# A two-layer hybrid trunk: the last two output-projection passes in the same PSUM banks, the mean square later, the sums of x earlier

## The chip, the cores and the metric

One core of a Trainium2 chip runs the whole program. The metric is device time in microseconds (us) of one execution, the median of several runs. A profile of one further execution shows what each engine did: PE (TensorE matmul), PEld (TensorE weight load), DVE (VectorE), ACT (ScalarE), POOL (GpSimd) and SP (SyncE, which issues most of the transfers).

## The reference

The input is one sequence of 512 frames with 1024 channels in float32. Two layers follow each other; cut to what matters here:

```python
def _layer(x, ...):                                # x: (1, 512, 1024)
    z = _rms(x, norm1) @ w_in                      # 1024 -> 2572 columns
    ya = sliding-window attention of 8 heads
    yb = forgetting attention of 4 heads
    yc = mLSTM readout of 4 heads
    x = x + concat(ya, yb, yc) @ w_out             # 1024 -> 1024
    u = _rms(x, norm2) @ w_ff1                     # 1024 -> 4096
    return x + square(relu(u)) @ w_ff2             # 4096 -> 1024
```

The change touches the product with `w_out`, the root-mean-square norm after it, and the order of work at the start of the feed-forward part.

## The kernel before, in words

x is kept transposed in SBUF as `xT`: 8 tiles of 128 channels by 512 frames. All large products run in float32 precision on fp32r operands: each operand is split into a rounded part and a rest (`whi`, `wlo` for weights, `xh`, `xl` for x), and each product is three matmuls, hi by hi (L263), hi by lo (L264) and lo by hi (L265).

**Weights come as jobs.** A job is 128 x 1024 elements: SP transfers them into a raw buffer (`raw`, `fraw`, `xt`, `ms`; L158), ACT rounds them to `whi` (L205), DVE subtracts to get `wlo` (L206). There are three `whi`/`wlo` buffers, so a job can be prepared at the earliest when the job three places ahead of it has been used up. `getjob` hands the jobs out in a fixed order.

**Attention and projections** are interleaved: `big_work` is a generator that emits a bit of projection work at each step, and `fill` and `fill_to(mark)` draw from it between pieces of attention work. The output projection is its last part. It contracts over eight tiles of 128 rows, k = 0 to 7. Tiles 0 to 3 belong to the sliding-window heads, 4 and 5 to the forgetting heads, 6 and 7 to the mLSTM heads, which come last. So it runs in three passes over k (`WPASS`: 0-3, 4-5, 6-7), each over four pairs of output tiles (`hf` = 0 to 3). For each pair it takes two PSUM banks, accumulates the pass and adds the two banks to `xT` on DVE (L587). In the third pass the sum is complete, and `xprep` follows for each tile: ACT makes the rounded part of x times the gain (L334), DVE the rest (L335). `c_tail(1)` transposes the last mLSTM readout on PE (L1007, four transposes of `yt`, which POOL writes at L1000), and ACT and DVE split the result into tile k = 7 (L1008, L1009).

**The feed-forward part.** Its hidden 4096 columns are made in eight rounds. A plain round (`ff1_std`, rounds 0 and 1, set by `NSTD = 2` in line 46) uses four jobs of 48 matmuls of 128 x 256. The other rounds (`ff1_st`) use a scheme with seven products of blocks in place of eight, and so seven jobs of 24 matmuls; the second matrix (`ff2`) uses the same scheme throughout. The seven products need sums and differences of blocks of x, which `xsums` forms on DVE and ACT (L354 to L375). The norm is not applied to x beforehand: since relu(r u) squared is r squared times relu(u) squared, DVE multiplies `xT` by the mean square plus epsilon before the first addition of a block (L1291), adds the products (L1292), and multiplies by r squared at the end of the layer. `sqacc` forms the sum of squares of `xT` (ACT squares, DVE adds at L330), and `emit_r2` averages it over channels with one PE product against a matrix of 1/1024 (L1123, float32, 512 columns), takes it out of PSUM on DVE (L1125) and derives r squared (ACT L1128, L1129; DVE L1130, L1131).

The first eight steps are the eight jobs of the two plain rounds; from the ninth on, `ff_pairs` alternates a job of `ff2` with one of `ff1_st`. In the text below the jobs of the feed-forward part are numbered from 0, so 0 to 7 are plain and 8 is the first of `ff2`. The sum of squares is emitted after job 0, `xsums` after jobs 1 to 4, the average after job 3. A scheduler orders the instructions of each engine; each engine then works through its list in that order.

## Time and profile before

| | |
|---|---|
| time, median of 3 runs (lowest to highest) | 1066.45 us (1066.31 to 1067.0) |
| the profiled execution: its own time / its span | 1067.08 us / 1065.4 us |
| PE busy, matmuls | 1055.0 us (99%), 8764 |
| PEld busy | 1004.0 us (94%) |
| DVE busy | 904.2 us (85%) |
| ACT busy | 629.5 us (59%) |
| granted PE clock | 0.999 |

The span runs from the first to the last instruction; the time holds about 1.7 us more. A busy share is time in which at least one instruction of the engine is under way. Matmuls overlap each other, so one that is listed with 0.28 us occupies PE for less: how long each one really takes from the next is read from the starts of neighbours, or from how many fit into a stretch. Layer 0 has its output projection up to about 223 us and its feed-forward part from there to 535 us; layer 1 follows 525.8 us later with the same order of work.

### The profile page before, as it was taken

Reading aid. Unit: us, or ns where it says so; the run is one execution under the profiler, and the core shown is the slowest. Engines: PE = TensorE matmul, PEld = TensorE weight load, DVE = VectorE, ACT = ScalarE, POOL = GpSimd, SP = SyncE. Lnnn points to the kernel's source line nnn. Section 1 sums busy time; section 2 is a strip of 40 time slices with the busy share of each in tenths; the row PEclk is TensorE's granted clock in tenths of the full one; section 3 lists DMA queues with packets and bytes.
Section 4 is the critical chain, followed back from the end, with each engine's and each line's share of the span. In section 5 each row is a group of like instructions: output and inputs, shape, how many; then the busy total and the mean of one; then the engine's idle time right before and its main releaser. Section 6 shows DMA issues by size and latency. Waiting matters only on the chain.

```text
span 1065.4 us, 21677 instructions
## 1 busy us (share of the span) xinstructions
PE 1055.0 (99%) x8764; PEld 1004.0 (94%) x8764; DVE 904.2 (85%) x1540; ACT 629.5 (59%) x1097; POOL 102.3 (10%) x154
## 2 busy tenths in 40 slices
PE   8999999999999999999999999999999999999998
PEld 8999977899999999999999998778999999999998
DVE  7696877899997988988977878688999888898797
ACT  6446655376666666567455467444766666666662
POOL 2030020100010000010001200101000101001000
PEclk9999999999999999999999999999999999999999
DMA  6523121165388587677135221213544876777742
GB/s 214 161 102 110 60 68 50 61 191 146 119 209 225 160 217 199 176 203 196 51 110 163 95 80 41 87 43 136 143 120 140 221 208 177 225 180 187 220 128 80
DMA packets 47365, 151.86 MB, mean 143 GB/s; under 512 B 5648, under 2 KB 8848, under 8 KB 47264
## 3 DMA queue, kind: packets, MB, share of 16 engines
q1 hardware_dynamic: 39056, 120.84, 33.1%
q0 software_dynamic: 8064, 29.36, 15.6%
q8 instruction: 69, 1.13, 0.4%
q14 instruction: 32, 0.26, 0.1%
q10 hardware_dynamic: 144, 0.26, 0.1%
HBM read 147.86 MB, written 2.13 MB: 141 GB/s over the span
## 4 chain that ended last, share of the span: by engine, by line
PE 89%; DVE 7%; ACT 2%; issue 1%; DMA 0%; SPq 0%; DVEq 0%
PE at L263 27%; PE at L264 26%; PE at L265 26%; DVE rt L726 2%; DVE wlo L206 1%; PE at L856 1%; PE at L898 1%; PE at L756 1%; PE at L881 1%; PE at L979 1%; DVE z L728 1%; DVE z L722 1%; PE at L811 1%; PE at L789 1%; DMA raw<-in_w_in_dram 0%
## 5 line engine op out<-in xcount | busy, mean ns | idle before, releaser
L205 ACT ACTIVATE whi<-raw 128x1024 fp32r<-128x1024 f32 (+1 forms) x130 | 136.4, 1049 | 114.9 <-PE at L264 88.2
L264 PE MATMUL at<-xhl,whi 128*128 128x256 f32 (+1 forms) x704 | 198.7, 282 | 0.0
L263 PE MATMUL at<-xhl,whi 128*128 128x256 f32 (+1 forms) x640 | 181.9, 284 | 0.0
L265 PE MATMUL at<-xhl,wlo 128*128 128x256 f32 (+1 forms) x640 | 181.1, 283 | 0.0
L263 PE MATMUL at<-yg,whi 128*128 128x256 f32 (+1 forms) x592 | 179.9, 307 | 0.5 <-DVE xT L1292 0.5
L206 DVE TENSOR_TENSOR wlo<-raw,whi 128x1024 fp32r<-128x1024 f32 (+1 forms) x130 | 157.0, 1208 | 27.3 <-ACT whi L205 26.9
L265 PE MATMUL at<-yg,wlo 128*128 128x256 f32 (+1 forms) x592 | 178.4, 301 | 0.0
L264 PE MATMUL at<-yg,whi 128*128 128x256 f32 (+1 forms) x560 | 169.4, 303 | 0.0
L263 PE MATMUL at<-whi,xhl 128*128 128x256 f32 (+1 forms) x576 | 162.9, 283 | 1.2 <-ACT xhl L334 1.0
L265 PE MATMUL at<-whi,xhl 128*128 128x256 f32 (+1 forms) x576 | 160.4, 279 | 0.5 <-DVE xhl L335 0.5
L264 PE MATMUL at<-wlo,xhl 128*128 128x256 f32 (+1 forms) x576 | 160.3, 278 | 0.5 <-DVE wlo L206 0.5
L205 ACT ACTIVATE whi<-fraw 128x1024 fp32r<-128x1024 f32 x100 | 106.3, 1063 | 89.3 <-PE at L264 79.8
L206 DVE TENSOR_TENSOR wlo<-fraw,whi 128x1024 fp32r<-128x1024 f32 x100 | 122.1, 1221 | 27.1 <-ACT whi L205 26.6
L264 PEld LDWEIGHTS at<-xhl,whi 128*128 128x128 f32 x704 | 132.1, 188 | 1.9 <-issue 0.5
L265 PEld LDWEIGHTS at<-xhl,wlo 128*128 128x128 f32 x640 | 120.7, 189 | 1.2
L263 PEld LDWEIGHTS at<-xhl,whi 128*128 128x128 f32 x640 | 120.1, 188 | 1.8 <-ACT ct L1230 0.5
L263 PEld LDWEIGHTS at<-yg,whi 128*128 128x128 f32 x592 | 111.2, 188 | 6.3 <-issue 1.7
L265 PEld LDWEIGHTS at<-yg,wlo 128*128 128x128 f32 x592 | 111.1, 188 | 5.3
L263 PEld LDWEIGHTS at<-whi,xhl 128*128 128x128 f32 x576 | 108.3, 188 | 2.2 <-ACT xhl L334 1.2
L264 PEld LDWEIGHTS at<-yg,whi 128*128 128x128 f32 x560 | 105.3, 188 | 4.2 <-DVE yg L1009 0.5
L265 PEld LDWEIGHTS at<-whi,xhl 128*128 128x128 f32 x576 | 108.2, 188 | 1.0 <-DVE xhl L335 0.9
L264 PEld LDWEIGHTS at<-wlo,xhl 128*128 128x128 f32 x576 | 108.2, 188 | 0.7 <-DVE wlo L206 0.7
(299 smaller groups left out, 2516.8 us busy)
## 6 DMA issues: line engine op xcount, KB each, us to landing
fraw<-in_w_dram SPq DMA_DIRECT2D x72, 512.0 KB, 4.3
raw<-in_w_dram SPq DMA_DIRECT2D x56, 512.0 KB, 4.3
raw<-in_w_in_dram SPq DMA_DIRECT2D x34, 512.0 KB, 3.3
fraw<-in_w_dram POOLq DMA_DIRECT2D x32, 512.0 KB, 6.2
raw<-in_w_out_dram SPq DMA_DIRECT2D x16, 512.0 KB, 3.2
xt<-in_w_dram SPq DMA_DIRECT2D x16, 512.0 KB, 5.8
raw<-in_w_dram POOLq DMA_DIRECT2D x14, 512.0 KB, 7.4
ms<-in_w_dram SPq DMA_DIRECT2D x12, 512.0 KB, 4.3
```

The lines of the kernel that those rows point to most:

```text
L205: A.activation(hi[:, cs_], raw[:, cs_], AF.Copy)
L206: V.tensor_tensor(lo[:, cs_], raw[:, cs_], hi[:, cs_], ALU.subtract)
L263: T.matmul(o, sh, mh, start=first, stop=False, skip_group_check=skip)
L264: T.matmul(o, sh, ml, start=False, stop=False, skip_group_check=skip)
L265: T.matmul(o, sl, mh, start=False, stop=last, skip_group_check=skip)
L722: V.tensor_tensor(z10, z10, bc(rq), ALU.mult)
L726: V.tensor_tensor(r10[:, oo:oo + n, a:a + 32], z10[:, oo:oo + n, b:b + 32], tb(S_, n, a, a + 32), ALU.mult)
L728: V.tensor_tensor(zaq[t], ro[:, :640], rt[:, :640], ALU.add)
L756: T.matmul(sc[r][:, g * 256:g * 256 + nk], qTA[g][r * 64:(r + 1) * 64, c * P:(c + 1) * P], kTA[r * 64:(r + 1) * 64, k0:k0 + nk], start=Tru ...
L789: T.transpose(pt[:w, u * P:(u + 1) * P], pe[:, u, :w], ident)
L811: T.matmul(po[r * 64:(r + 1) * 64, g * P:(g + 1) * P], vt[:w, r * 64:(r + 1) * 64], p1[:w, u * P:(u + 1) * P], start=g == 0, stop=p2 is No ...
L856: T.matmul(sp[:, :nk], qTB[rs, pr, n * P:(n + 1) * P], kTB[rs, pr, :nk], start=True, stop=False)
```

## The change

Four things are altered, in both layers.

- **Output projection.** The first pass (k = 0 to 3) stays. The second and third share banks: pairs 0, 1 and 2 take k = 4 and 5, keep their six banks open, and take k = 6 and 7 later, in the order 2, 0, 1; pair 3 takes k = 4 to 7 at one go, last. Each pair is added to `xT` once for the two passes. The weights are laid out on the host so that the four jobs fit this order.
- **The last transposes** (`c_tail(1)`) come after k = 4 and 5 of pairs 0 and 1, no longer after those of all four pairs.
- **Sums of x first.** `xsums` is emitted after jobs 0 to 3, the sum of squares after job 4, the average (`emit_r2`) after job 7. The buffer `xt`, in which `xsums` works, goes to the weight transfers after job 4 in place of job 7. The last two operations on r squared (`finish_r2`) move behind the first seven products of `ff2`.
- **Bank choice.** `bank(True)`, used where ACT writes a bank before PE accumulates into it, takes a bank that has been used in this part before.

In words the change was also said to use one plain round of the first feed-forward matrix in place of two. In the code `NSTD` is 2 on both sides; the new loop is written with `NSTD`, and its value doesn't change.

```diff
@@ -570,26 +570,54 @@
                         DEST[gname](t, ps[t])
                 done.add(gname)
                 yield 1.31
-            for pi, (a, b) in enumerate(WPASS):
-                for hf in range(4):
-                    ps = [att() for _ in range(2)]
-                    if b - a == 4 or hf % 2 == 0:
-                        ws = getjob()
-                    for k in range(a, b):
-                        hi, lo = ws[k - a if b - a == 4 else hf % 2 * 2 + k - a]
-                        for j in range(2):
-                            cs_ = slice(j * P, (j + 1) * P)
-                            mm3(ps[j], hi[:, cs_], lo[:, cs_], yhi(k), ylo(k), k == a, k == b - 1)
-                        if k < b - 1:
-                            yield 1.31
-                    for j in range(2):
-                        kx = hf * 2 + j
-                        V.tensor_tensor(xT[:, kx], ps[j], xT[:, kx], ALU.add)
-                        if pi == len(WPASS) - 1:
-                            xprep(kx, g2(l, kx), xh, xl)
-                    if hf == 3:
-                        done.add(f"wo{pi}")
+            def wo_part(ps, tiles, k, first, stop):
+                hi, lo = tiles
+                for j in range(2):
+                    cs_ = slice(j * P, (j + 1) * P)
+                    mm3(ps[j], hi[:, cs_], lo[:, cs_], yhi(k), ylo(k), first, stop)
+
+            def wo_out(ps, hf, full):
+                for j in range(2):
+                    kx = hf * 2 + j
+                    V.tensor_tensor(xT[:, kx], ps[j], xT[:, kx], ALU.add)
+                    if full:
+                        xprep(kx, g2(l, kx), xh, xl)
+
+            for hf in range(4):
+                ps = [att() for _ in range(2)]
+                ws = getjob()
+                for k in range(4):
+                    wo_part(ps, ws[k], k, k == 0, k == 3)
+                    if k < 3:
+                        yield 1.31
+                wo_out(ps, hf, False)
+                if hf == 3:
+                    done.add("wo0")
+                yield 1.31
+            open_ = {}
+            for hf in range(3):
+                open_[hf] = [att() for _ in range(2)]
+                if hf != 1:
+                    ws = getjob()
+                for k in (4, 5):
+                    wo_part(open_[hf], ws[2 * (hf % 2) + k - 4], k, k == 4, False)
+                    if k == 5:
+                        done.add(f"wo1{hf}")
                     yield 1.31
+            for hf in (2, 0, 1, 3):
+                if hf == 3:
+                    open_[hf] = [att() for _ in range(2)]
+                if hf in (0, 3):
+                    ws = getjob()
+                for k in range(4 if hf == 3 else 6, 8):
+                    wo_part(open_[hf], ws[k - 4 if hf == 3 else (hf if hf < 2 else 1) * 2 + k - 6], k, hf == 3 and k == 4,
+                            k == 7)
+                    if k < 7:
+                        yield 1.31
+                wo_out(open_[hf], hf, True)
+                if hf == 3:
+                    done.add("wo2")
+                yield 1.31
         bw = big_work()
         credit = [0.0]
@@ -1091,8 +1119,9 @@
             fill(FB, "wo0")
         fill_to("wo0")
         c_tail(0)
-        fill_to("wo1")
+        fill_to("wo11")
         c_tail(1)
+        fill_to("wo12")
         close_phase()
         open_phase(FFP)
         pos["ff"] = l
@@ -1113,8 +1142,13 @@
         quads = [unit(xb(0, 1, t_)) for t_ in (xh, xl)]
         banks = deque(att() for _ in range(8))
-        def bank():
-            return banks.popleft()
+        full = set()
+
+        def bank(seeded=False):
+            b = next(b for b in banks if not seeded or id(b) in full)
+            banks.remove(b)
+            full.add(id(b))
+            return b
         rr_ = {}
@@ -1127,9 +1161,12 @@
             r2 = cst.tile([P, S], F32, tag="aux", name=f"r2{l}")
             A.activation(lnv, nv, AF.Ln, scale=-1.0)
             A.activation(r2, lnv, AF.Exp, scale=-1.0)
+            rr_.update(nv=nv, lnv=lnv, r2=r2)
+
+        def finish_r2():
+            nv, lnv, r2 = (rr_[n] for n in ("nv", "lnv", "r2"))
             V.tensor_tensor(lnv, nv, r2, ALU.mult)
             V.scalar_tensor_tensor(r2, lnv, 2.0, r2, ALU.add, ALU.mult)
-            rr_.update(nv=nv, r2=r2)
         def prod(bk, bh, bl, start, halves=None):
             ws = getjob()
...
@@ -1351,28 +1388,27 @@
                         xprep(kx, g1(l + 1, kx), xhA, xlA)
                 give(s, dg, "t")
                 if s == 0 and dg:
+                    finish_r2()
                     free_ff.append(ms_)
                 yield
         gens = {1: (None for r in range(NR) for _ in (ff1_std if r < NSTD else ff1_st)(r // 2, r % 2)),
                 2: (None for s in range(NS) for _ in ff2(s))}
         bg = None
-        for n_ in range(4 * NSTD):
-            next(gens[1])
+        for n_, (which, u) in enumerate([(1, None)] * 4 * NSTD + list(ff_pairs())):
+            next(gens[which])
             if n_ == 0:
+                xt_ = wt("xt", "xt")
+                bg = xsums(l, *(v3(xt_[:, i * S:(i + 1) * S], 256) for i in range(2)))
+            if n_ < 4:
+                next(bg)
+                next(bg)
+            if n_ == 4:
                 for kx in range(KT):
                     sqacc(kx, kx == 0)
-            if n_ == 3:
+                free_ff.append(xt_)
+            if n_ == 7:
                 emit_r2()
-            if n_ == 1:
-                xt_ = wt("xt", "xt")
-                bg = xsums(l, *(v3(xt_[:, i * S:(i + 1) * S], 256) for i in range(2)))
-            if bg is not None:
-                next(bg, None)
-                next(bg, None)
-        free_ff.append(xt_)
-        for which, u in ff_pairs():
-            next(gens[which])
         close_phase()
         free_ff.clear()
...
```

How the scheduler orders it shows in three places of layer 0. In the names, `at` is a PSUM bank, `yg` holds the readouts y, `yt` the last mLSTM readout before its transposes, `accs` the sums of squares, `ones_m` the matrix of 1/1024, `ms` the buffer that takes the mean square. The numbers behind a name tell tiles apart and mean nothing else.

**PE, end of the output projection.** Before, the transposes L1007 stand behind the last matmul of the second pass for pair 3 (banks 2837 and 2838):

```order
L263 MATMUL at_2838<-yg,whi_2624 128x512
L264 MATMUL at_2838<-yg,whi_2624 128x512
L265 MATMUL at_2838<-yg,wlo_2625 128x512
L1007 MATMUL at_2853<-ident,yt_2695 128x128 x4
L263 MATMUL at_2870<-yg,whi_2781 128x512
```

Now (as L1035) behind the last one for pair 1 (banks 2798 and 2799), and pair 2 follows:

```order
L264 MATMUL at_2798<-yg,whi_2442 128x512
L265 MATMUL at_2798<-yg,wlo_2443 128x512
L264 MATMUL at_2799<-yg,whi_2442 128x512
L265 MATMUL at_2799<-yg,wlo_2443 128x512
L1035 MATMUL at_2812<-ident,yt_2695 128x128 x4
L263 MATMUL at_2819<-yg,whi_2624 128x512
```

The transposes have moved 24 matmuls of 512 columns ahead.

**PE, plain rounds.** Before, the average L1123 stands after job 3, 192 matmuls of 256 columns behind the first of the feed-forward part:

```order
L263 MATMUL at_2968<-xhl,whi_3042 128x256
L264 MATMUL at_2968<-xhl,whi_3042 128x256
L265 MATMUL at_2968<-xhl,wlo_3043 128x256
L1123 MATMUL at_2969<-accs_3026,ones_m 128x512
L263 MATMUL at_2970<-xhl,whi_3113 128x256
```

Now (as L1157) after job 7, 384 matmuls behind it, with the first job of `ff2` next (`gx` holds its operand):

```order
L263 MATMUL at_2956<-xhl,whi_3296 128x256
L264 MATMUL at_2956<-xhl,whi_3296 128x256
L265 MATMUL at_2956<-xhl,wlo_3297 128x256
L1157 MATMUL at_2949<-accs_3279,ones_m 128x512
L263 MATMUL at_2950<-gx_2845,whi_3356 128x256
```

The average has moved 192 matmuls back; the list of PE holds as many rows as before (8139), and no other matmul of this part has changed its place.

**DVE, where the average is read.** Before, the read L1125 is followed by the rests of jobs 6, 7 and 8 (`wlo_3252`, `wlo_3319`, `wlo_3378`), with the first multiplications of `xT` by the mean square (L1291) behind job 7's; a part of the list reads:

```order
L1125 TENSOR_SCALAR ms_2865<-at_2969 128x512
L206 TENSOR_TENSOR wlo_3252<-fraw_2869,whi_3251 128x1024
L356 SCALAR_TENSOR_TENSOR xbx_2866<-xt_3102,xbx_2866 128x512
L1199 SCALAR_TENSOR_TENSOR ct_2868<-ct_2868 128x512
```

Now the read (L1159) stands between the rests of jobs 9 and 10, and the first multiplication (L1328) and the first addition of a product (L1329) ahead of job 11's (`ct` holds hidden columns):

```order
L206 TENSOR_TENSOR wlo_3409<-fraw_2847,whi_3408 128x1024
L216 TENSOR_TENSOR fraw_2847<-raw_74,fraw_2847 128x1024
L1159 TENSOR_SCALAR ms_2843<-at_2949 128x512
L206 TENSOR_TENSOR wlo_3473<-fraw_2847,whi_3472 128x1024
L1236 SCALAR_TENSOR_TENSOR ct_2846<-ct_2846 128x512
L1237 TENSOR_TENSOR ct_2846<-ct_2846 128x512
L1328 SCALAR_TENSOR_TENSOR xT<-xT,ms_2843 128x2x256
L1221 TENSOR_TENSOR yg<-ct_2846,yg 128x1024 x2
L1329 TENSOR_TENSOR xT<-xT,at_2950 128x2x256
L206 TENSOR_TENSOR wlo_3503<-raw_74,whi_3502 128x1024
```

All eight multiplications, which stood ahead of the rest of job 10 before, now stand behind it, between the weight preparations of jobs 10 to 22.

9 lines of the change are left out of this document (5 added, 4 removed).

## The prediction

> **What bounds the kernel now.** I read the page's first part and the chain of waits, then busy time by windows around the three places of the change, then single instructions there.
>
> ```profile
> span 1065.4 us, 21677 instructions
> PE 1055.0 (99%) x8764; PEld 1004.0 (94%) x8764; DVE 904.2 (85%) x1540; ACT 629.5 (59%) x1097; POOL 102.3 (10%) x154
> PE 89%; DVE 7%; ACT 2%; issue 1%; DMA 0%; SPq 0%; DVEq 0%
> ```
>
> The first line of shares is busy time, the second is the chain that ended last. PE has nine tenths of it, so the time is the sum of the matmuls plus a little waiting. In the windows around the change (busy us of PE, PEld, DVE, ACT, POOL, then clock, DMA share, GB/s) there is no waiting at all:
>
> ```profile
> 200.00:225.00 25.00, 25.00 (x132) 20.56 (x131) 22.38 (x38) 13.30 (x23) 3.07 (x9) 1.00 0.47 168
> 225.00:250.00 25.00, 25.00 (x210) 24.52 (x209) 24.61 (x41) 18.35 (x29) 1.07 (x2) 1.00 0.52 131
> 250.00:275.00 25.00, 25.00 (x223) 25.00 (x222) 24.16 (x32) 16.48 (x21) 1.72 (x2) 1.00 0.49 123
> ```
>
> PE is full in all three and DVE close behind it: 24.61 and 24.16 of 25. So DVE work that goes away gains nothing, and DVE work that comes at a worse moment can cost. One thing stands out. The second window holds 210 matmuls, the third 223. The counts don't come from waits, so I cut the windows at the average L1123, 192 plain matmuls ahead of it and 192 behind, in both layers:
>
> ```profile
> 223.02:245.64 22.62, 22.62 (x193) 22.61 (x192) 22.23 (x38) 15.97 (x26) 1.88 (x2) 1.00 0.56 142
> 246.86:268.61 21.75, 21.75 (x194) 21.75 (x193) 21.75 (x29) 13.29 (x18) 1.72 (x2) 1.00 0.52 122
> ...
> 748.80:771.42 22.62, 22.62 (x193) 22.61 (x192) 22.25 (x38) 15.98 (x26) 1.75 (x2) 1.00 0.53 143
> 772.64:794.39 21.75, 21.75 (x194) 21.75 (x193) 21.75 (x29) 13.29 (x18) 1.75 (x2) 1.00 0.51 122
> ```
>
> The same 192 matmuls of 256 columns take 22.61 us ahead of the average and 21.75 behind it: 117.8 and 113.3 ns each, at a granted clock of 1.00 in all four. I call them the slow and the fast pitch. The change of pitch falls on the average itself:
>
> ```profile
> 245.41 0.28 PE L264 MATMUL at<-xhl,whi 128*128 128x256 f32 x1
> 245.52 0.28 PE L265 MATMUL at<-xhl,wlo 128*128 128x256 f32 x1
> 245.64 1.02 PE L1123 MATMUL at<-accs,ones_m 128*128 128x512 f32 x2
> 246.10 0.68 PE L263 MATMUL at<-xhl,whi 128*128 128x256 f32 x1
> 246.62 0.28 PE L264 MATMUL at<-xhl,whi 128*128 128x256 f32 x1
> 246.74 0.28 PE L265 MATMUL at<-xhl,wlo 128*128 128x256 f32 x1
> 246.86 0.28 PE L263 MATMUL at<-xhl,whi 128*128 128x256 f32 x1
> 246.97 0.28 PE L264 MATMUL at<-xhl,whi 128*128 128x256 f32 x1
> ```
>
> The average is the only float32 product here, and the slow pitch ended with it in both layers, 525.8 us apart. What starts or ends the slow pitch the trace doesn't say.
>
> **The change part by part.**
>
> *The plain round* is not removed: `NSTD` is 2 on both sides and the list of PE keeps its length. Had one gone, four jobs of 48 would have become seven of 24, and (192 - 168) x 0.1133 x 2 layers = 5.4 us would have been saved. It counts 0.
>
> *The average goes behind job 7.* It costs what it cost, 245.64 to 246.51 beyond a normal step. But if the slow pitch lasts until a float32 product passes, it now lasts for 384 matmuls: 192 more at 22.61 instead of 21.75, that is 0.86 us per layer, **+1.7 us** in two. Bounds: 0, if something else that stays where it was ended it; and the slow pitch for the rest of the part, if the average doesn't end it in its new place:
>
> ```profile
> 314.90:531.90 217.00, 217.00 (x1918) 1.00 0.66 180
> ```
>
> 1918 x 4.5 ns = 8.6 us per layer, 17.3 in two. Below nothing: if the slow pitch isn't entered, 2 x 0.86 = 1.7 us are gained. I take the first, as the one that both flips of this trace bear out.
>
> The Trainium skill, "TensorE: Matmul & The Clock Gate", section "Wait — 56ns, not 53.3ns?", gives one warm start-to-start time, columns over 2.4 GHz plus about 2.5 ns; my estimate from it for 256 columns is 109.2 ns. The trace disagrees: 113.3 and 117.8 ns at full clock. By that rule no product could alter the pitch, and the move would be free; that is the second rival below.
>
> *Eight additions per layer fall away* (L587), worth 8 x 0.60 = 4.8 us of DVE:
>
> ```profile
> L587 DVE TENSOR_TENSOR xT<-at,xT 128x512 f32<-128x512 f32 x17 | 11.0, 682 | 2.2 <-PE at L265 2.2
> ```
>
> Of DVE's idle time, 2.2 us stand directly ahead of this line and are waits for PE: 0 gained. PE's back-to-back matmuls hide it. Without that cover each would cost its 0.68 us.
>
> *The transposes come 24 matmuls earlier*: 24 x 0.2267 (the 512-column step, 222.57 to 222.80) = 5.44 us, from 211.58 to 206.14. Their operand comes from POOL:
>
> ```profile
> 205.03 1.17 POOL L1000 TENSOR_TENSOR yt<-hs,co 128x64 f32<-128x64 f32 x4 [3.95 <-DVE hs L996]
> ...
> 211.58 0.60 PE L1007 MATMUL at<-ident,yt 128*128 128x128 f32 x4
> 211.93 0.48 PE L263 MATMUL at<-yg,whi 128*128 128x512 f32 x1
> ...
> 214.53 0.49 PE L264 MATMUL at<-yg,whi 128*128 128x512 f32 x1
> 214.86 0.40 PE L265 MATMUL at<-yg,wlo 128*128 128x512 f32 x1
> ...
> 222.57 0.39 PE L264 MATMUL at<-yg,whi 128*128 128x512 f32 x1
> 222.80 0.39 PE L265 MATMUL at<-yg,wlo 128*128 128x512 f32 x1
> ```
>
> POOL's four pieces are done at 206.20, so the last is 0.06 us late if the first transpose needed it. But each transpose waits for its own piece, and the last starts about 0.3 us after the first. Bounds 0 to 0.35 per layer (all four behind the last piece); I take 0.05, **+0.1**. If PE stalls there, matmuls behind it wait, nobody else. In return the wait for the rest of tile 7 goes: 214.53 to 214.86 is 0.33 in place of 0.227, 0.1 per layer, **-0.2** in two, for the 12 matmuls of pair 2 (2.7 us) and its k = 6 now stand between.
>
> *The sums of x move ahead of the sum of squares* on a DVE that PE doesn't wait for in that stretch: 0. Its cover is the stock of prepared jobs, and that is where a loss could come from. The eight multiplications by the mean square move from ahead of job 10's rest to behind it. Let e be the end of job 7 (before: 268.28). The DVE list behind the average's read starts with the hidden columns of job 7, which ACT finished here:
>
> ```profile
> 269.95 1.06 ACT L1232 ACTIVATE ct<-ct 128x1024 f32<-128x1024 f32 x1
> ...
> 271.87 0.68 DVE L1199 SCALAR_TENSOR_TENSOR ct<-ct 128x512 f32<-128x512 f32 x1
> 272.47 0.68 DVE L1200 TENSOR_TENSOR ct<-ct 128x512 f32<-128x512 f32 x1
> ...
> 281.68 1.22 DVE L206 TENSOR_TENSOR wlo<-fraw,whi 128x1024 fp32r<-128x1024 f32 x1
> 282.81 1.22 DVE L220 TENSOR_TENSOR fraw<-raw,fraw 128x1024 f32<-128x1024 f32 x1
> 283.95 0.68 DVE L1292 TENSOR_TENSOR xT<-xT,at 128x512 f32<-128x512 f32 x1
> ...
> 311.37 1.22 DVE L206 TENSOR_TENSOR wlo<-fraw,whi 128x1024 fp32r<-128x1024 f32 x1
> ```
>
> 269.95 + 1.06 is e + 2.7. From there to the rest of job 25 the new list has 26 rows of 512 elements and 24 of 1024. Start to start these take 0.60 and 1.14 (the rows above), 43.0 together; with 1.22 for the rest itself it is there at e + 46.9. PE wants it as third matmul of job 25: 0.87 for the average, 17 jobs of 24 x 0.1133 = 46.2, 0.2 for two matmuls, about e + 47.2 with a little for the signal. Slack **0.3 us**; before it was 312.59 against 314.52 and 0.2, about 2 us. If each row took its listed 0.68 and 1.22, 47.0 in place of 43.0, it would be 3.7 us late. I take 0, nearest to the rows of this stretch, which do follow each other at 0.60 and 1.14.
>
> *The order of pairs, banks and weight jobs* changes neither the number of matmuls nor of transfers: 0; its cover is the same stock of jobs.
>
> Sum: 1.7 + 0.1 - 0.2 = **+1.6 us**. The profiled execution goes from 1067.08 to 1068.7. It stands 0.6 above the median, so the median goes from 1066.45 to about **1068.0**.
>
> **The rivals.**
>
> *Pitch goes its own way.* Something at that time, not the average, ended the slow pitch: the narrow sums of x on DVE, say, whose last is done there too:
>
> ```profile
> 245.34 0.88 DVE L369 SCALAR_TENSOR_TENSOR xt<-xT,pcol,xt 128x256 f32<-128x256 f32 x2
> 246.13 0.68 DVE L358 TENSOR_TENSOR xbx<-xt,xbx 128x512 fp32r<-128x512 f32 x1
> ```
>
> For it: 246.2 is within 0.6 us of the flip, and no row names a cause. Against: the pitch is slow from the first plain matmul at 223.0, a job and more before the first of these sums is emitted, and it changes exactly at L1123. The sums now come a job (5.6 us, some 48 matmuls) earlier, which would even gain 48 x 4.5 ns = 0.2 per layer; without that it is 0.1 - 0.2. About 1066.3 by the median.
>
> *The slow pitch isn't entered.* It began where 512 columns gave way to 256, and what stands ahead of that is changed (the transposes are farther off, pair 3 runs k = 4 to 7 at one go). -1.7 - 0.1: 1064.6.
>
> *Late rests, the slower side.* At one place, the DVE list behind the average's read, more rows than PE gives time for. It decides from 0.3 us of extra DVE time in 47 on, less than one row: a rounding by ACT that comes late, or rows at 0.62 in place of 0.60, would do. For it: DVE is busy 24.16 of 25 now. Against: this trace's rows run without gaps. About 1 us per layer more, 1070; at the full 3.7, 1075.4, which needs every row at its listed length and is therefore unlikely.
>
> *The slow pitch doesn't end at the average.* Either because it needs another cause, or because a late rest starts it again. One such stall stands in the trace (0.5 us; columns are total, times, longest):
>
> ```profile
> PE at L263 <- DVE xT L1292: 0.5, 1, 0.5
> ```
>
> Then 1.6 + 17.3: about 1085.
>
> **How the numbers follow.** Two tenths of a per cent, 2.13 us, is about what a measurement of this kernel can tell from no change. The sum stands: 0.52, 1068.0, itself between 1067.3 and 1068.6 (bounds of transposes and of the removed wait). Pitch as before: 0.17, 1066.3. Late rests: 0.15, 1069 to 1071.5. Slow pitch for the rest: 0.09, 1085. Not entered: 0.07, 1064.6. The range of 8 in 10 takes the first three, 1066.0 to 1070.5, leaving out the last two and the upper part of the late rests. Faster means below 1064.3: less than half of the last case, 0.03. Slower means above 1068.6: late rests, the slow pitch for the rest and the very edge of the first, 0.26. The same: 0.71.
>
> **What would show it.** Right: 192 plain matmuls in 22.6 us ahead of job 4 and again in 22.6 behind it, in both layers, and 21.75 for as many behind L1157; transposes near 206.2 with no row of waits of PE for `yt` above 0.1; no row of waits of PE for `wlo` L206. Wrong: a pitch that changes inside the plain jobs or not at L1157; waits of PE for `wlo` between 290 and 335 us; or PE's busy time lower by more than 1 us.

## The result and the profile after

The changed kernel takes 1081.18 us (1078.8 to 1082.66, five runs) against 1066.86 (1066.31 to 1067.34, five runs): 1.0129 times as long, 95% interval 1.0119 to 1.014. That is 14.3 us more where 1.6 were forecast, and outside the range of 1066.0 to 1070.5. The profiled execution took 1078.8 us, with this span and busy time:

```profile
span 1076.7 us, 21663 instructions
PE 1066.8 (99%) x8764; PEld 1016.0 (94%) x8764; DVE 894.5 (83%) x1524; ACT 626.3 (58%) x1097; POOL 102.8 (10%) x154
```

The matmuls are as many as before, 8764, and PE is busy 11.8 us longer with them (1066.8 against 1055.0), while DVE is busy 9.7 us less. So the time isn't in idle stretches. The windows of PE alone show where it is (busy us and matmuls of PE, clock, DMA share, GB/s): the plain jobs of layer 0, the first jobs behind the average, and then 220 us of each layer's feed-forward part.

```profile
222.60:267.71 45.11, 45.11 (x385) 1.00 0.55 139
268.92:303.84 34.92, 34.92 (x311) 1.00 0.46 123
306.00:526.00 220.00, 220.00 (x1870) 1.00 0.70 187
841.20:1061.20 220.00, 220.00 (x1944) 1.00 0.70 189
```

The plain jobs are slow for 384 matmuls, as forecast. Behind the average PE is fast for some 310. From 306 us on layer 0 does only 1870 matmuls in 220 us, and layer 1 does 1944 of the same in the same time: 117.7 against 113.2 ns, at one and the same clock. So layer 0 fell back into the slow pitch near 304 us and stayed there to its end, and layer 1, in this execution, did not. PE's list shows what happened there, first in layer 0, then in layer 1:

```profile
303.84 0.28 PE L264 MATMUL at<-yg,whi 128*128 128x256 f32 x1
303.95 0.28 PE L265 MATMUL at<-yg,wlo 128*128 128x256 f32 x1
304.18 0.36 PE L263 MATMUL at<-xbx,whi 128*128 128x256 f32 x1
304.37 0.28 PE L264 MATMUL at<-xbx,whi 128*128 128x256 f32 x1
...
839.33 0.28 PE L265 MATMUL at<-yg,wlo 128*128 128x256 f32 x1
840.64 0.36 PE L263 MATMUL at<-xbx,whi 128*128 128x256 f32 x1 [1.03 <-DVE ct L1305]
840.84 0.28 PE L264 MATMUL at<-xbx,whi 128*128 128x256 f32 x1
```

At the first matmul of job 21 PE comes 0.11 us late in layer 0 (303.95 to 304.18, where 0.11 is a normal step) and 1.2 us late in layer 1. The line of waits names DVE's L1305. Job 21 adds its product to a bank whose sum so far L1305 must first read, and on DVE that read stood behind a multiplication by the mean square (L1328) and the weights' rests:

```profile
296.93 1.23 DVE L220 TENSOR_TENSOR fraw<-fraw 128x1024 f32<-128x1024 f32 x1 [0.17 <-DMA fraw<-in_w_dram]
...
301.60 1.22 DVE L206 TENSOR_TENSOR wlo<-fraw,whi 128x1024 fp32r<-128x1024 f32 x1
302.74 0.69 DVE L1328 SCALAR_TENSOR_TENSOR xT<-xT,ms 128x512 f32<-128x512 f32 x1
303.34 0.69 DVE L1305 TENSOR_TENSOR ct<-at,ct 128x512 f32<-128x512 f32 x1
...
833.39 1.23 DVE L220 TENSOR_TENSOR fraw<-fraw 128x1024 f32<-128x1024 f32 x1 [1.26 <-DMA fraw<-in_w_dram]
...
839.21 0.68 DVE L1328 SCALAR_TENSOR_TENSOR xT<-xT,ms 128x512 f32<-128x512 f32 x1
839.81 0.68 DVE L1305 TENSOR_TENSOR ct<-at,ct 128x512 f32<-128x512 f32 x1
```

In layer 0 L1305 ended at 304.03, and PE wanted it at 304.06 less the way of the signal; in both layers PE's matmul starts 0.15 us after that end. DVE had waited 0.17 us for a transfer there. In layer 1 it had waited 1.26 us, and L1305 ended at 840.49 instead of about 839.4.

The profiled execution's 11.3 us of longer span add up so: the feed-forward part begins 0.4 earlier (222.60 against 223.03); 192 more matmuls at the slow pitch in each layer, 2 x 0.86; some 2040 matmuls at the slow pitch behind the wait in layer 0, 2040 x 4.45 ns = 9.1; the two waits, 0.1 and 1.2. That makes 11.7. Two things take off 0.5: before has a step of 0.22 near the end of layer 0 (at 532.01) with 22 slow matmuls behind it, some 0.3 us that the change doesn't spend, and the stretch from there to the feed-forward part of layer 1 is 0.2 shorter. The median run is 2.4 us above the profiled one; of that one there is no trace, and it isn't accounted for here.

### The profile page after: what moved, and what is told of

Its sections match the earlier page's. It is cut to its first block, busy times and chain, and to the rows that moved or that the text cites. A ratio compares the mean times of both kernels' runs of the same rounds, so it can differ in the third digit from the quotient of the medians.

```text
span 1076.7 us, 21663 instructions
## 1 busy us (share of the span) xinstructions
PE 1066.8 (99%) x8764; PEld 1016.0 (94%) x8764; DVE 894.5 (83%) x1524; ACT 626.3 (58%) x1097; POOL 102.8 (10%) x154
## 4 chain that ended last, share of the span: by engine, by line
PE 83%; DVE 11%; ACT 3%; issue 2%; DMA 1%; SPq 0%; DVEq 0%
PE at L263 25%; PE at L265 25%; PE at L264 25%; DVE wlo L206 2%; DVE rt L754 2%; PE at L884 1%; PE at L926 1%; PE at L909 1%; ACT pe L797 1%; PE at L1007 1%; DMA fraw<-in_w_dram 1%; DVE z L750 1%; DVE z L756 1%; PE at L784 1%; DMA raw<-in_w_in_dram 0%
## 5 line engine op out<-in xcount | busy, mean ns | idle before, releaser
L205 ACT ACTIVATE whi<-raw 128x1024 fp32r<-128x1024 f32 (+1 forms) x136 | 142.4, 1047 | 114.6 <-PE at L264 87.0
L206 DVE TENSOR_TENSOR wlo<-raw,whi 128x1024 fp32r<-128x1024 f32 (+1 forms) x136 | 164.7, 1211 | 35.9 <-ACT whi L205 35.6
```

The costliest lines, as they stand in the source:

```text
L205: A.activation(hi[:, cs_], raw[:, cs_], AF.Copy)
L206: V.tensor_tensor(lo[:, cs_], raw[:, cs_], hi[:, cs_], ALU.subtract)
```

## The experiments

A wait of 0.1 us that costs 9 us was a reason to look at the pitch itself. The theory: the average's late place makes DVE late near job 21, PE waits, and the wait brings the slow pitch, which then stays. Of its parts each can be tried alone. Times of "before" are those of the same group of runs. With two pitches per layer, the times of one kernel can fall into groups some 10 us apart; where they do, the groups are told. Only one execution of each run has a trace. The diffs are cut to what matters; where the kernel calls a small helper for the added product, the product is written out.

**The average alone, late (before, with one number changed).**

```diff
-            if n_ == 3:
+            if n_ == 7:
                 emit_r2()
```

> The kernel before, with the average alone moved from behind job 3 to behind job 7; output projection, sums of x and sum of squares stay as they were. Theory (a float32 product ends the slow pitch, a short wait of PE starts it again, and the late multiplications make DVE late for a bank that PE wants in job 21): 192 plain matmuls in 22.6 us ahead of job 4 and again behind it, fast behind the average, then a wait of PE for DVE's read of a bank near job 21 and the slow pitch behind it; 1075 to 1085. Rival (the average's place costs only the longer slow pitch, the rest comes from the output projection or from the sums): +1.7, 1068.6, and no wait of PE near job 21.

Measured: 1069.75, three times 1079.3 to 1079.8, and twice 1089.1 to 1089.2, before 1066.75. The groups lie 9.6 us apart, which fits none, one or both layers in the slow pitch for the rest of the layer. The profile is of the slowest and shows both; the other two groups have no trace. PE's list in layer 0:

```profile
277.14 0.28 PE L264 MATMUL at<-gx,whi 128*128 128x256 f32 x1
277.71 0.38 PE L265 MATMUL at<-xbx,wlo 128*128 128x256 f32 x1 [0.30 <-DVE wlo L206]
```

Behind this wait both layers have 2125 matmuls in 250 us, 117.6 ns each (windows of PE):

```profile
280.00:530.00 250.00, 250.00 (x2125) 1.00 0.68 182
816.00:1066.00 250.00, 250.00 (x2125) 1.00 0.68 182
```

So the average's place alone is enough to lose what the change lost, though not in each execution. Here the wait is for the rest of job 11, three jobs behind the average and not at job 21.

**All but the average's place (the change, with squares, average and sums where they were).**

The three conditions are those of the sums of x, the squares and the average. Not shown: `xsums` begins after job 1, `xt` goes to the weights after job 7 and `finish_r2` leaves its later place, all as before.

```diff
-            if n_ < 4:
+            if 1 <= n_ < 5:
                 next(bg)
                 next(bg)
-            if n_ == 4:
+            if n_ == 0:
                 for kx in range(KT):
                     sqacc(kx, kx == 0)
-            if n_ == 7:
+            if n_ == 3:
                 emit_r2()
+                finish_r2()
```

> The changed kernel with sums of squares, average and sums of x back in their old places; of the change only the output projection's new order, the choice of banks and the weights' layout are left. Theory (everything that was lost hangs on the average's place): 192 plain matmuls in 22.6 us ahead of the average, fast for the whole rest of the part; a little under before for the shorter wait at tile 7, 1066.0 to 1066.9. Rival (the new banks or pairs cause the wait): slower than 1070.

Measured: 1066.57 (1066.09 to 1067.01, eleven runs), ratio 0.9998 (0.999 to 1.0007). The output projection's new order and the choice of banks together are worth nothing that can be measured, and cost nothing.

**Without the multiplications (the change, `L1328` left out).**

```diff
-            if s == 0 and (dg, i, j) not in seen:
-                seen.add((dg, i, j))
-                V.scalar_tensor_tensor(t_, t_, -1.0, bc_("nv"), ALU.mult, ALU.mult)
```

> The changed kernel without the eight multiplications of xT by the mean square in each layer: they are left out, so the two layers add unscaled values, and the time is that of the rest. Theory (DVE's late multiplications make PE wait near job 21, and the wait starts the slow pitch): no wait of PE for DVE between jobs 8 and 30, slow for the 384 plain matmuls, fast for the whole rest; before plus 1.7 for the plain ones minus 0.2, 1067.8 to 1068.6. Rival (the wait comes from the new choice of banks or from elsewhere in the list): the wait and the slow pitch stay, above 1075.

Measured: 1068.62 against 1067.0, ten of eleven runs between 1068.09 and 1068.86, one at 1077.65. PE's windows, the plain jobs and then 260 us of each layer:

```profile
222.60:267.40 44.80, 44.80 (x382) 1.00 0.54 136
268.90:528.90 260.00, 260.00 (x2297) 1.00 0.65 179
795.40:1055.40 260.00, 260.00 (x2296) 1.00 0.65 179
```

The first window is slow (117.3 ns), the other two are fast to the end (113.2). With 0.60 us of DVE less, eight times per layer, the change costs +1.6 us: the prediction's own sum, for a DVE that is in time. The one run at 1077.65 has no trace.

**A break without any wait (before, one float32 product of 128 columns behind job 21).**

```diff
             prod1(X, 6, False)
+            if (s, rr) == (1, 0):
+                T.matmul(banks[0][:, :P], ones_m, ones_m, start=True, stop=True)
```

> The kernel before with one float32 product of 128 columns, whose result nobody reads, behind job 21 of each layer; the list of DVE is row for row that of before, and PE waits for nothing there. Theory (any break in the run of like matmuls, not a wait alone, can bring the other pitch, as a product of this shape did at full speed with three others in the run before): the slow pitch from there to the end of the layer, about 2190 matmuls by 4.45 ns in each layer, 9.7, so 1066.7 + 0.4 + 19.5 = 1086.6; 1077 if it does so in one layer only. Rival (only late work of other engines brings the slow pitch): 0.4 more, 1067.2.

Measured: 1085.07 (1084.76 to 1085.4, five runs), 18.1 us above before, for two products of 0.2 us. PE's windows ahead of the product and behind it, in both layers:

```profile
250.00:300.00 50.00, 50.00 (x444) 1.00 0.46 130
310.00:360.00 50.00, 50.00 (x427) 1.00 0.74 197
790.00:840.00 50.00, 50.00 (x444) 1.00 0.53 147
850.00:900.00 50.00, 50.00 (x427) 1.00 0.74 194
```

444 matmuls in 50 us ahead, 427 behind, and no wait of PE is listed there. So the slow pitch needs no late engine: a break in PE's own stream can bring it, and here it lasts for the 2000 matmuls to the end of the layer.

**The same product ahead of the plain jobs (before).**

```diff
+        T.matmul(banks[0][:, :P], ones_m, ones_m, start=True, stop=True)
         for n_ in range(4 * NSTD):
```

> The kernel before with one float32 product of 128 columns, whose result nobody reads, ahead of the first plain matmul of each layer. Theory (a float32 product ends the slow pitch): the 192 plain matmuls ahead of the average take 21.75 us in place of 22.61, 0.86 less per layer against 0.22 for the product: 1066.9 - 1.7 + 0.4 = 1065.5. Rival (the pitch there follows from the work around it): 0.4 us more, 1067.3.

Measured: 1065.63 against 1066.75, 0.9991 (0.9982 to 0.9999). The plain jobs are fast from the start (179 matmuls in 20 us):

```profile
223.40:243.40 20.00, 20.00 (x179) 1.00 0.59 153
```

And the average, which now meets the fast pitch, leaves it fast. By this run a float32 product could be what ends the slow pitch. The run above, in which the same product brought it, and the next one say otherwise.

**The same product behind each seventh job of the six rounds (the change).**

```diff
             prod1(X, 6, False)
+            T.matmul(banks[0][:, :P], ones_m, ones_m, start=True, stop=True)
```

> The changed kernel with one float32 product of 128 columns, whose result nobody reads, behind each seventh job of the six rounds with seven products (12 in all, the first right behind the job ahead of which PE waited). Theory (a float32 product ends the slow pitch): the wait stays, the slow pitch behind it lasts 24 matmuls only, and the 12 products cost about 0.22 us each, 2.6 together; from 1081.2 some 9 to 17 go: 1068 to 1073. Rival (the pitch follows from what other engines do at that time): 2.6 us more, about 1084.

Measured: 1081.95 (1080.29 to 1084.54), as slow as without. Neither theory had this: behind each of the twelve products the pitch is the other one. Three windows between successive products of layer 0:

```profile
308.00:344.00 36.00, 36.00 (x320) 1.00 0.87 242
346.00:384.00 38.00, 38.00 (x325) 1.00 0.67 169
387.00:422.00 35.00, 35.00 (x312) 1.00 0.76 212
```

112.5, 116.9 and 112.2 ns; a window also counts the matmuls that it cuts at its ends, and by their starts it is 113.3, 117.8 and 113.3. This shape turns the pitch round.

**The shape of the average behind job 21 (the change).** The product has 512 columns.

```diff
             prod1(X, 6, False)
+            if (s, rr) == (1, 0):
+                T.matmul(banks[0], ones_m, rr_["r2"], start=True, stop=True)
```

> The changed kernel with one float32 product of 512 columns, the shape of the average, behind job 21 of each layer, right behind the wait; its result is read by nobody. So far a product of this shape was followed by the fast pitch every time, from slow (eight times) and from fast (twice). Theory (this shape leaves the fast pitch whatever was before): about 2 x 0.85 for the products, the waits of about 1 us stay, no slow pitch from job 22 on: 1069.5 to 1072. Rival (it turns the pitch round, or it is a draw): one or both layers slow, 1079 to 1090.

Measured: 1082.93 (1082.03 to 1083.69). In the profile the product followed slow with slow in layer 0 and fast with fast in layer 1. So this shape doesn't always leave the fast pitch. The average has the same shape: in the traces of all the runs it met the slow pitch 23 times and left the fast one 22 times; once, in the run with one plain round and two breaks further down (layer 1, at 782.12), the slow one stayed.

**Eleven kinds of break, one after the other (before).** One product whose result is not read stands behind nearly every job from 22 on, of the next kind in `BR` (1 is float32, 0 is bfloat16).

```diff
+BR = [(0, 32), (0, 64), (0, 128), (1, 256), (1, 64), (1, 384), (1, 128), (0, 96), (1, 32), (1, 512), (1, 192)]
             next(gens[which])
+            if m_ >= 14 and len(banks) >= 2:
+                T.matmul(banks[0][:, :w_], ..., start=True, stop=True)
```

> The kernel before with a small product, whose result nobody reads, behind nearly every job from job 22 on, in turn of 32, 64, 128 and 96 columns in bfloat16 and 32 to 512 columns in float32; the list of DVE is that of before. Read from the trace: which pitch the 24 matmuls between two such products have. If a break turns the pitch round, it changes at each; if the width or the kind of the break sets it, the same break is always followed by the same pitch; if it is a draw, neither. From the runs so far 128 columns of float32 turned it round each time but one, 512 columns gave the fast one ten times and the slow one twice: I expect the gap in time that the break leaves to decide, so the same kind behind the same pitch gives the same result in more than 9 of 10. The time itself tells little: the products cost some 20 to 30 us and half of the matmuls are slow, 1095 to 1110.

Measured: 1122.1 us, one execution, 12 above what was expected; the time was not the point. From the starts of the matmuls between two breaks (only their medians are used), in both layers:

| break | pitch before -> after | times |
|---|---|---|
| float32, 32 columns | fast -> fast | 15 |
| float32, 64 | fast -> slow; fast -> fast | 14; 1 |
| float32, 128 | slow -> fast; fast -> slow | 14; 1 |
| float32, 192 | fast -> fast | 14 |
| float32, 256 | fast -> fast | 15 |
| float32, 384 | slow -> slow; fast -> fast | 14; 1 |
| float32, 512 | fast -> fast | 15 |
| bfloat16, 32, 64, 128 | fast -> fast | 45 |
| bfloat16, 96 | fast -> fast; slow -> fast | 14; 1 |

The single fast -> fast at 64 columns is the last break of layer 0, with other work behind it. Apart from it, the same kind of break behind the same pitch was followed by the same pitch each time: in this order of breaks it is no draw. The order is fixed, though, so nearly each break has the same one ahead of it, and eight of the eleven kinds met the fast pitch alone. That kind and pitch decide everywhere isn't shown; the 512-column product of the other runs speaks against it. The starts at one break of 64 columns:

```profile
319.74 0.28 PE L265 MATMUL at<-yg,wlo 128*128 128x256 f32 x1
319.85 0.33 PE L1384 MATMUL at<-r,ones_m 128*128 128x64 f32 x2
319.99 0.36 PE L263 MATMUL at<-xbx,whi 128*128 128x256 f32 x1
320.19 0.28 PE L264 MATMUL at<-xbx,whi 128*128 128x256 f32 x1
320.31 0.28 PE L265 MATMUL at<-xbx,wlo 128*128 128x256 f32 x1
```

Ahead of it a step is 0.11, behind it 0.12 (medians 113 and 118 ns).

**The change with the wait, but without the slow pitch.** Four bfloat16 products of 96 columns in each layer, the first ahead of job 0.

```diff
+        T.matmul(banks[0][:, :96], identb, identb[:, :96], start=True, stop=True)
         for n_, (which, u) in enumerate([(1, None)] * 4 * NSTD + list(ff_pairs())):
...
+            if n_ in (21, 23, 26):
+                T.matmul(banks[0][:, :96], identb, identb[:, :96], start=True, stop=True)
```

> The changed kernel with four products of 96 columns in bfloat16 in each layer, whose results nobody reads: ahead of the first plain matmul and behind jobs 21, 23 and 26. In the run with many breaks such a product was followed by the fast pitch each of 15 times, once from the slow one; it costs about 0.13 us. Theory (the change lost its time to the slow pitch and 1 to 2.6 us to the waits themselves): fast from the first plain matmul on, the wait ahead of job 21 stays; 1066.9 - 0.2 - 1.7 + 8 x 0.13 + 1 to 2.6 = 1067 to 1068.6. Rival (the loss is in the late work itself, and the pitch only goes with it): above 1075.

Measured: 1070.88 (1068.97 to 1071.49) against 1066.7. Both layers are fast throughout, 1942 matmuls in 220 us:

```profile
305.00:525.00 220.00, 220.00 (x1942) 1.00 0.70 189
833.00:1053.00 220.00, 220.00 (x1942) 1.00 0.70 188
```

The waits of PE (us in total, times, longest) still hold the read that job 21 needs, L1308 here:

```profile
PE at L263 <- DVE ct L1308: 2.9, 2, 1.5
```

Against its own before the kernel is 4.2 us slower in place of 14.3, so 10.1 us are back, though PE still waits. It is 2.3 above what was expected, because the waits are longer: ahead of job 21 1.6 us beyond a step in each layer in place of 0.1 and 1.2, and for a rest just before it 0.6 and 0.1. With fast plain jobs PE is there 1.7 us earlier, and DVE is not. What was gained ahead of the wait was given back in it.

One thing this profile doesn't show: by the starts, the pitch behind the two waits of 1.6 us is fast already, ahead of the product behind job 21. So a wait needn't bring the slow pitch, and none was there for the three later products to end. That a product of 96 columns can end it is seen twice: once in the run before this one, and once in the run with one plain round and five breaks (at 272.38, 117.8 ns ahead and 113.5 behind).

**The average one job earlier (the change).**

```diff
-            if n_ == 7:
+            if n_ == 6:
                 emit_r2()
```

> The changed kernel with the average behind job 6 in place of job 7, all else alike. DVE may then begin the multiplications 48 matmuls, 5.5 us, earlier, about as much as eight of them take (8 x 0.60 = 4.8). Theory (the slack near job 21 is short by 0.1 to 1.2 us): no wait there, slow for 336 plain matmuls, 1066.9 - 0.2 + 144 x 2 x 0.00445 = 1068.0. Rival (the eight multiplications keep their places behind the rests whenever the average comes): the wait stays, 1078 to 1090.

Measured: 1077.32 to 1078.31 three times, 1085.97 to 1087.88 three times. The theory was right that the wait at job 21 goes, and wrong about the time. Both layers are slow from job 11 on, in a profile whose waits of PE hold nothing of that place. The list of PE there, in layer 0:

```profile
276.88 0.28 PE L264 MATMUL at<-xbx,whi 128*128 128x256 f32 x1
276.99 0.32 PE L265 MATMUL at<-xbx,wlo 128*128 128x256 f32 x1
277.14 0.28 PE L263 MATMUL at<-xbx,whi 128*128 128x256 f32 x1
```

DVE's list has the rest that the second of these reads:

```profile
275.64 1.22 DVE L206 TENSOR_TENSOR wlo<-raw,whi 128x1024 fp32r<-128x1024 f32 x1
```

And the windows of PE behind it, 250 us of each layer:

```profile
277.10:527.10 250.00, 250.00 (x2125) 1.00 0.68 184
813.30:1063.30 250.00, 250.00 (x2124) 1.00 0.67 182
```

The rest of job 11 ends at 276.86, the matmul that reads it starts at 276.99 and is listed with 0.32 in place of 0.28, and the next starts 0.152 later in place of 0.113. A hitch of 0.04 us, put down to no one, and then 2125 slow matmuls in 250 us. That the rest's late end makes the hitch is likely by these times, not shown.

**The multiplications on POOL (the change).** The sign goes into the first addition.

```diff
-                V.scalar_tensor_tensor(t_, t_, -1.0, bc_("nv"), ALU.mult, ALU.mult)
-            V.tensor_tensor(t_, t_, q2(bk), ALU.subtract if i else ALU.add)
+                G.tensor_tensor(t_, t_, bc_("nv"), ALU.mult)
+                V.scalar_tensor_tensor(t_, t_, -1.0, q2(bk), ALU.mult, ALU.subtract if i else ALU.add)
+            else:
+                V.tensor_tensor(t_, t_, q2(bk), ALU.subtract if i else ALU.add)
```

> The changed kernel with the eight multiplications by the mean square moved from DVE to POOL (the sign goes into the first addition on DVE, which stays one instruction); the result is the reference's. Theory (without them DVE is in time, as in the run that leaves them out): no wait of PE near job 21, slow for 384 plain matmuls and fast for the rest, 1068 to 1069. Rival (POOL's access slows DVE, or a multiplication comes late on POOL): waits of PE for DVE remain and the slow pitch comes, 1077 to 1088.

Measured: 1081.41 to 1098.27, median 1090.97; the profile is of the slowest. The rival came true: while POOL works, DVE is slowed. POOL's list (start, duration of all eight):

```profile
269.24 16.11 POOL L1328 TENSOR_TENSOR xT<-xT,ms 128x512 f32<-128x512 f32 x8 [8.69 <-DVE ms L1159]
```

DVE's list in that time:

```profile
270.14 1.79 DVE L1236 SCALAR_TENSOR_TENSOR ct<-ct 128x512 f32<-128x512 f32 x1
...
273.56 0.68 DVE L1329 SCALAR_TENSOR_TENSOR xT<-xT,at 128x512 f32<-128x512 f32 x1
...
278.02 2.28 DVE L206 TENSOR_TENSOR wlo<-raw,whi 128x1024 fp32r<-128x1024 f32 x1
```

And of PE's waits (total, times, longest):

```profile
PE at L265 <- DVE wlo L206: 7.2, 2, 3.6
```

Operations of 0.68 take 1.79 and those of 1.22 take 2.28, and PE waits 3.6 us for a rest in each layer. Of the rows shown only L1329, one of whose operands is a PSUM bank, keeps its 0.68. Behind the long wait there is a cost of another kind. PE's windows there, one in each layer, have a granted clock of 0.50:

```profile
280.40:283.40 3.00, 3.00 (x14) 0.50 0.56 175
823.00:826.30 3.30, 3.30 (x18) 0.50 0.38 146
```

A matmul takes 0.21 us from the next there, in place of 0.11, which costs some 1.5 us in each layer. Only behind that, at the wait for L1305, does the slow pitch begin in this execution. So this run adds up waits, half clock and slow pitch, and isn't a test of the pitch alone.

**One plain round (the change, with what its words announce).**

```diff
-NSTD = 2
+NSTD = 1
-    LEAD = 0
+    LEAD = 7
```

> The changed kernel with what the words of the change announce and its code does not do: one plain round (NSTD = 1), and the seven jobs of the next round ahead of the first job of the second matrix (LEAD = 7). 192 plain matmuls become 168 in each layer: 48 x 0.1133 = 5.4 us less matmul time, and the slow pitch ahead of the average is now 192 + 96 long. If DVE keeps up: 1066.7 - 5.4 + 0.9 = 1062.2. If DVE is late as in the changed kernel, the slow pitch comes in one or both layers: 1071 to 1082.

Measured: 1064.19 to 1064.89 five times, 1073.92 to 1075.18 four times, 1085.11 to 1085.46 three times; before 1067.0. The fast group is 2.6 us under before. The slowest has the trace, with both layers in the slow pitch from about job 11 on; the middle one fits one layer. With the multiplications on POOL as well:

> One plain round, and the eight multiplications on POOL. The run with one plain round had times in three groups, near 1064.5, 1074.7 and 1085.2, with waits of PE for DVE of 0.3 to 0.6 us each. Theory (DVE's load makes the waits): fewer waits, 1062 to 1064.5 with the fast pitch from the average or the last wait on. Rival (the waits come from the sums or the rests, not from the multiplications): the three groups stay.

Measured: 1079.27 to 1091.06, median 1090.48, with 10.5 us of waits for rests, DVE operations of 1.7 to 1.8 and 2.3 us beside POOL's, and a clock of 0.50 behind three of the four waits. With a break of 96 columns ahead of job 0 and behind jobs 10, 12, 14 and 18:

> One plain round, with five products of 96 columns in bfloat16 in each layer: ahead of the first plain matmul and behind jobs 10, 12, 14 and 18. Theory (the three groups 1064.4, 1074.7 and 1085.2 are none, one or both layers in the slow pitch): one group, near 1064.4 + 10 x 0.13 - 2.1 for the plain matmuls = 1063.6. Rival (another cause makes the groups): three groups remain, about 1.3 higher.

Measured: 1065.9 (1065.53 to 1066.64, eleven runs), 0.9993 (0.9985 to 1.0002). The three groups are one. It is 2.3 above what was expected: with the early break PE comes sooner to a bank that ACT fills (L1286), and the longest wait there is listed with 1.2 us, where it was 0.3; that is 1.8 in the two layers, and the rest isn't accounted for. And with two breaks only, behind jobs 12 and 14:

> One plain round, with two products of 96 columns in bfloat16 in each layer, behind jobs 12 and 14, whose results nobody reads; none ahead of the first plain matmul. Theory (the slow pitch that makes the groups begins with the waits near job 11, and a break behind them ends it): one group near the fast one of 1064.4, plus 4 x 0.13 and a little for the slow stretch between the wait and the break, 1064.9 to 1065.3. Rival (a later wait brings it again, or the first break meets the phase that it turns to slow): a second group 10 higher remains.

Measured: 1065.23 to 1066.13 six times, 1073.81 to 1074.12 five times, 1082.97 once. The rival came true. Behind the last break each layer still has a hitch, at 307.93 and at 833.30, again about 0.04 us:

```profile
307.93 0.31 PE L265 MATMUL at<-xhl,wlo 128*128 128x256 f32 x1
308.08 0.29 PE L263 MATMUL at<-xhl,whi 128*128 128x256 f32 x1
...
833.30 0.32 PE L265 MATMUL at<-xhl,wlo 128*128 128x256 f32 x1
833.46 0.28 PE L263 MATMUL at<-xhl,whi 128*128 128x256 f32 x1
```

From the starts, the first is 37 ns and is followed by over 1950 fast matmuls, the second 47 ns and by as many at the slow pitch.

**The best of the pieces.** The output projection of the change, average, squares and sums in their old places, one float32 product of 128 columns ahead of job 0.

> The changed kernel with the average, the sums and the squares back in their old places and one float32 product of 128 columns ahead of the first plain matmul of each layer. Theory: the pieces add, 1066.6 for the first and 1.1 less for the second: 1065.5, the fast pitch from the first plain matmul on. If the product ahead meets another phase than in the kernel before, the plain matmuls stay slow: 1067.0.

Measured: 1065.28 (1064.7 to 1065.94, eleven runs) against 1066.86, 0.9987 (0.9979 to 0.9996). It is 1.6 us faster than before, and all eleven runs lie below before's median.

## Why the prediction was wrong

*The slow pitch on the plain jobs* was right in size and place: 384 slow matmuls in both layers, fast behind L1157. Where DVE was in time (the run without multiplications), the whole change cost +1.6 us, the forecast sum. The transposes at 205.8 to 206.2 and the shorter wait at tile 7 were right within a few tenths: the feed-forward part begins 0.4 earlier, where less than 0.1 was forecast. So each sign that was named as showing the prediction right came (the one listed wait for a rest, 0.3 us, lies in the projections and stands in before with 0.5), and none of those that were to show it wrong: they looked for waits for rests, and the wait was for a bank.

*A slow pitch that lasts until a float32 product passes* was a rule from two flips, and wrong as a rule, though it held for the average in the place that the change gave it. The pitch behaves as a state of PE's stream. A product of another shape, a wait, or a hitch of 0.04 us can change it, and the first two have done so in both directions: 128 columns turned it round, 384 kept it, 64 brought the slow one.

*"I take 0" for the late rests* is the step that failed. The slack of 0.3 us was worked out at one place, the rest of job 25, by rows at 0.60 and 1.14, and the same sum applies to every place at which PE needs DVE. The read of job 21's bank (L1305) has the same slack: 18 rows of 1024 and 21 of 512 up to it are 2.7 + 20.5 + 12.6 + 0.1 = e + 35.9, wanted at e + 0.87 + 13 jobs x 2.72 = e + 36.2 less the signal. Measured, it was there at e + 36.2 in layer 0 and PE was 0.11 late: 0.15 of the slack is the signal, and DVE's row began 0.1 later and waited 0.17 for a transfer. I had looked at rests only. A slack of 0.3 us in 47 was then counted as safe with 0.52 against 0.15, though a transfer that lands 1.26 us late, as in layer 1, uses it up.

*The price of a late operation* was wrong by far more. I put about 1 us per layer on it, the wait itself. The wait itself was 0.1 and 1.2 us; what it starts is 2040 matmuls by 4.45 ns, 9.1 us. That combination stood among the rivals ("a late rest starts it again", about 1085) with 0.09. By the runs above it should have had about half of what the late rests had. Four traces have ten such waits behind the average (the change, the average alone late, the product behind each seventh job, the four breaks of 96 columns): five brought the slow pitch and five left the fast one. The stall that was quoted there has the fast pitch behind it (ten matmuls, to the end of the part); the step of 0.22 at 532.01, in the same trace, has the slow one behind it and wasn't seen. Which of the two a wait brings isn't known.

*One pitch for all*: the Trainium skill, "TensorE: Matmul & The Clock Gate", section "Wait — 56ns, not 53.3ns?", gives one start-to-start time once warm. Here two stand side by side with the clock at 1.00 in both, 113.3 and 117.8 ns, and the measurements decide. (The prediction calls this its second rival; the free move is the first in its list.)

That the chosen place of the average was the cause, and the output projection was not, is shown by the two runs that have each alone; the new places of the sums and squares of x weren't tried alone. Why the slow pitch costs 4.45 ns per matmul, and which gap brings which pitch, stays open; so does why a 512-column product left slow behind slow twice, once as the average and once behind job 21.

## What to carry to other kernels

Where PE is full, compare matmuls per window of like work, not busy shares: a slow stretch and a fast one both read 100%. Where an engine behind PE has a few tenths of a microsecond of slack, work it out at each place at which PE needs it, and price a miss by what PE's stream may do afterwards, not by the length of the wait alone. When one kernel's times fall into groups, look for a state that lasts from a small event to the next one.

## What was not expected of the hardware

PE has at least two lasting pitches for the same 256-column matmuls, 113.3 and 117.8 ns at a granted clock of 1.00. In one fixed order of breaks the transition was repeatable (14 of 15 for 64 columns, 15 of 15 for 128 and 384), and a change of pitch can follow a hitch of 0.04 us that no line of waits shows. A product of 0.2 us therefore cost 9 us in one place and gained 0.6 net in another. And POOL's eight multiplications of 2.0 us each lengthened DVE's operations on SBUF from 0.68 to 1.79 us while they ran. Behind PE's waits of 3.6 us there the granted clock was 0.50 for some 3 us, a cost that the list of waits doesn't hold.
